# A constant tile of 64 bytes in place of 32: the left pools of an encoder block start 32 bytes later

## The chip, the cores and the metric

The kernel runs on one core of one Trainium2 chip. The metric is the device time of one execution in microseconds (us); lower is better. Three runs of the kernel before took 3334.75, 3335.2 and 3336.52 us, so the median is 3335.2 us.

## What is computed

One layer of a streaming encoder over x of 2048 tokens by 1024 features, all in float32. A projection feeds chunk-band attention and an RWKV-7 recurrence; the two are gated, merged and projected; then comes a feed-forward block. Cut to what matters here:

```python
h = rms_norm(x, pre_mix_g)
proj = h @ w_in                       # 1024 -> 5376
y_a = chunk_band_attention(q, k, v)   # from proj
y_b = rwkv7_time_mix(...)             # from proj
merged = sigmoid(gA) * (y_a @ proj_a) + sigmoid(gB) * (y_b @ proj_b)
x = x + rms_norm(merged @ w_out, post_mix_g)
hf = rms_norm(x, pre_ffn_g)
u = square(relu(hf @ w_up)) @ w_down  # 1024 -> 4096 -> 1024
x = x + rms_norm(u, post_ffn_g)
```

## The kernel before

**Products.** Every large product is made of three passes over operands that are split into a high and a low part (`split`, L76 and L77: ACT casts the high part, DVE subtracts it to get the low part). `mm3` (L85) issues, for each block of 128 along the contraction, high x high, high x low and low x high. Each pass is one MATMUL with a stationary operand of 128x128 (loaded by a LDWEIGHTS, the row PEld of the profile) and a moving operand of 128x512 float32. In a row of the profile the tile that is loaded as weights and the tile that streams stand in no fixed order, so the text says which is which.

**Order of the work.** The tokens are cut into four groups of 512. For each group the kernel runs the RWKV part, the attention part and the merge (`phase_rwkv`, `phase_attention`, `phase_merge`), all with the w_in, proj_a, proj_b and w_out products. Then the feed-forward runs in two halves of two groups each: `phase_up(0)`, `phase_down(0)`, `phase_up(1)`, `phase_down(1)`. Each of the four takes about 320 to 340 us.

**The up phase** (`phase_up`) works in 16 rows, each with two 128-column blocks of w_up on both halves of the contraction. A row is a scheme of seven products in place of eight, each of 12 matmuls (`product`): A11 and A12 against `bh`, `bl` (the normed input, `first_half`), and S2, S3, S1, S4, A22 against prepared combinations of the input, the tiles `t1`, `t2`, `t3`, `t4`, `b22`, each with an h and an l part. The weights (`a1h`, `s12h`, `s3h`, `s4h` and their l parts) are stationary; `bh`, `bl` and the t tiles stream. In each half the A11 and A12 products of the first eight rows are made ahead. In half 0 the rows from number 6 on also carry the steps of `residuals`, whose transposes (`ps_ht`, L1110) PE makes between products.

**The down phase** (`phase_down`) multiplies the squared activations by w_down: four plain blocks at each end (rows `ps_dn<-fop`: both operands lie in one tile) and between them 21 sums of products, each of 48 matmuls (rows `ps_dn<-fop,fop`: the stationary tile is `fop` from the pool z, the moving tile is `fop2` from the pool b).

**Where the tiles lie.** Pools are taken from one stack that grows upward (the left side) and one that grows downward from the top (`side="right"`). The left stack begins with the pool "const" (L160): `ident` (512 bytes in each partition), `g2c` (8 float32, 32 bytes) and `nhalf` (32 bytes). Everything in later left pools starts after these. On the left lie, among others, `whi` and `wlo` of the w_in stage, `hh`, `hl`, `mh`, `ml`, all t tiles, the pool z, and the pool b of half 0. On the right lie the operand pools of the up phase (`ops`, `ops1`: `a1`, `s12`, `s3`, `s4`), the pool `b1` (the place of `bh`, `bl` and of `fop2` in half 1), the attention's `ya`, and constants of the mixing stage.

These lines choose the side:

```python
            pt = u.enter_context(tc.tile_pool(name="ffp", bufs=2, space=PSUM, reuse_waits="tile"))
            self.phase_up(
                0, zp, rp, cb, pn, bpool(u, "ops", side="right"), 8, {},
...
                self.bp = bpool(ctx, "b1", side="right")
                self.sp = bpool(ahead, "ops1", side="right")
```

In the built program the steps between the blocks of one tile are 512 bytes for a stationary operand and 2048 bytes for a moving one, so all products of one pair of tiles have the same distance modulo 256. "Offset" below is the start of the moving operand minus the start of the stationary operand that is loaded while it streams (that of the following product), modulo 256.

Of the kernel before, what the change touches and what calls it, by code (L numbers as in the profile page):

```python
# [8 lines left out]
F32 = mybir.dt.float32  # L9
# [8 lines left out]
P = 128  # L18
D = 1024
KB = D // P  # L20
# [25 lines left out]
def advance(steps, n=None):  # L46

    while n is None or n > 0:
        if next(steps, steps) is steps:
            return  # L50
        n = n and n - 1


class Block:
# [102 lines left out]
    def constants(self, ctx, mixing):  # L157
        tc, nc, a = self.tc, self.nc, self.a
        keep = ctx.enter_context(tc.tile_pool(name="const", bufs=1))
# [1 line left out]
        dp = ctx.enter_context(tc.tile_pool(name="scratch", bufs=1, space=DRAM))  # L161
        self.ident = keep.tile([P, P], F32, name="ident")
        make_identity(nc, self.ident)
        self.g2c = keep.tile([P, KB], F32, name="g2c")
        self.nhalf = keep.tile([P, 8], F32, name="nhalf")
        nc.vector.memset(self.nhalf, -0.5)
        self.bones = cp.tile([P, P], F32, name="bones")
# [1351 lines left out]
    def run(self):  # L1519
        tc, e = self.tc, None  # L1520
        with ExitStack() as ctx, ExitStack() as mixing:
            e = mixing.enter_context
            consts = self.constants(ctx, mixing)
            advance(consts, 1)
            self.first = {}
            self.pd = ctx.enter_context(tc.tile_pool(name="pd", bufs=2, space=PSUM))
            self.wp = e(tc.tile_pool(name="w", bufs=2))
            self.hp = e(tc.tile_pool(name="h", bufs=1))
            with tc.tile_pool(name="p0", bufs=2, reuse_waits="tile") as sp, \
                 tc.tile_pool(name="p0p", bufs=2, space=PSUM, reuse_waits="tile") as pt:  # L1530
                self.phase_norm(0, sp, pt)
            advance(consts)
            self.order, self.feed = [], self.ahead()
            for g in range(self.NG):
                self.g = g
                self.phase_rwkv(g)
                self.phase_attention(g)
                with ExitStack() as c:
                    early = iter(())
                    if g == self.NG - 1:  # L1540
                        early = self.combinations(0, c.enter_context(tc.tile_pool(name="p1", bufs=1, reuse_waits="tile")), 2)
                    sp = c.enter_context(tc.tile_pool(name="p0", bufs=2, reuse_waits="tile"))
                    pt = c.enter_context(tc.tile_pool(name="p0p", bufs=2, space=PSUM, reuse_waits="tile"))
                    o = [sp.tile([P, D], F32, tag="o", bufs=GT, name=f"o{t}") for t in range(GT)]
                    self.phase_merge(g, o, self.after(g, sp, pt), early)
                    for t in range(GT):
                        self.nc.scalar.dma_start(self.od[g][t], o[t])
            mixing.close()
            e = ctx.enter_context
            zp = e(tc.tile_pool(name="z", bufs=2, reuse_waits="tile"))  # L1550
            rp = e(tc.tile_pool(name="raw", bufs=4, side="right", reuse_waits="tile"))
            cb = e(tc.tile_pool(name="cb", bufs=3, side="right", reuse_waits="tile"))
            pn = e(tc.tile_pool(name="ffpd", bufs=4, space=PSUM, reuse_waits="tile"))

            def bpool(ctx, name, **kw):
                return ctx.enter_context(tc.tile_pool(name=name, bufs=1, reuse_waits="tile", **kw))

            ahead = ExitStack()

            def nxt(loaded):  # L1560
                self.bp = bpool(ctx, "b1", side="right")
                self.sp = bpool(ahead, "ops1", side="right")
                load, parts = self.up_raw(rp), self.up_parts(self.sp)
                for i in range(2):
                    self.made[i] = self.up_first(i, load, parts)
                return self.first_half(2, self.bp, loaded)

            self.made = {}
            with ExitStack() as c:
                bp = bpool(c, "b")  # L1570
                advance(self.first_half(0, bp))
                with self.nc.allow_non_contiguous_dma(reason="one vector"):
                    self.nc.gpsimd.dma_start(self.g2c, self.a["pre_ffn_g"].rearrange("(k p) -> p k", p=P))
                with ExitStack() as u:
                    pt = u.enter_context(tc.tile_pool(name="ffp", bufs=2, space=PSUM, reuse_waits="tile"))
                    self.phase_up(
                        0, zp, rp, cb, pn, bpool(u, "ops", side="right"), 8, {},
                        lambda z, mp: self.residuals(z, mp, cb, pt),
                    )
                self.phase_down(0, zp, bp, rp, cb, pn, nxt)  # L1580
            self.phase_up(1, zp, rp, cb, pn, self.sp, 8, self.made)
            ahead.close()
            self.phase_down(1, zp, self.bp, rp, cb, pn)
# [44 lines left out]
```

## Time and profile before

| | |
|---|---|
| median of three runs | 3335.2 us |
| the profiled execution, its own time | 3334.86 us |
| its span, first to last instruction | 3333.2 us |
| mean granted TensorE clock | 0.994 |
| busy share of PE, PEld, DVE, ACT, POOL | 97%, 77%, 68%, 47%, 12% |

The span is the time between the first and the last instruction; 1.7 us of the execution lie outside it. PE is TensorE's products, PEld its weight loads, which run beside the products. DVE, ACT and POOL are the vector, scalar and GpSimd engines; SP only issues DMAs. A row of the listing by line and form gives the line, the engine, the operation, the output and input tiles, the shapes, the count, the busy time in us, the mean duration of one in ns, and the idle time of the engine just before these instructions with what ended it. Busy time is the union of the instructions' times: matmuls overlap in the records, so the busy time divided by the count is the step from one to the next, and the mean duration is longer than that step.

### The profile page before, as it was taken

To read this page: it belongs to the slowest core of one execution; us is meant where nothing else is said; L and a number is where in the kernel's file an instruction comes from. 1 tells how busy PE (TensorE), PEld (TensorE's weight loads), DVE (VectorE), ACT (ScalarE), POOL (GpSimd) and SP (SyncE) were. 2 spreads that over 40 slices of the span, in tenths; PEclk is the share of its full clock that TensorE was granted. 3 is DMA by queue.
4 is the path that set the end of the run, shared out by engine and by line. 5 is a ranking of instruction groups with operands and counts; after the bars stand their busy time and mean duration, and the time that the engine had idled before them with its cause. 6 is when DMAs were issued, how large, how long until landed. Compare 5 with 4: busy or idle time off the path is not lost. (4 is left out here: it accounts for less than half of the span.)

```text
span 3333.2 us, 49202 instructions
## 1 busy us (share of the span) xinstructions
PE 3236.2 (97%) x18945; PEld 2578.1 (77%) x18945; DVE 2271.5 (68%) x3782; ACT 1571.5 (47%) x2551; POOL 386.6 (12%) x757
## 2 busy tenths in 40 slices
PE   7999999999999999999999999999999999999998
PEld 6877787877777877778777777778788877887887
DVE  6784557765566765666775665777678978776687
ACT  4535534445644444645444635466443454454332
POOL 2110011101021011021111000133000111100001
PEclk9999999999999999999999999999999999999999
DMA  5224343225273234273224266566455564543443
GB/s 157 90 89 148 106 143 108 73 93 179 89 244 120 64 105 169 84 240 127 77 96 154 72 230 215 191 235 229 175 189 202 177 225 168 169 164 134 158 151 126
DMA packets 165874, 497.29 MB, mean 149 GB/s; under 512 B 18108, under 2 KB 26496, under 8 KB 160264
## 3 DMA queue, kind: packets, MB, share of 16 engines
q1 hardware_dynamic: 106740, 357.78, 32.5%
q0 software_dynamic: 22688, 77.61, 6.1%
q10 hardware_dynamic: 36212, 58.76, 4.8%
q8 instruction: 149, 2.44, 0.3%
q14 instruction: 85, 0.70, 0.1%
HBM read 365.08 MB, written 132.15 MB: 149 GB/s over the span
## 5 line engine op out<-in xcount | busy, mean ns | idle before, releaser
L85 PE MATMUL psd<-hh,whi 128*128 128x512 f32 x1344 | 542.0, 403 | 6.1 <-ACT whi L76 3.9
L85 PE MATMUL psd<-hl,whi 128*128 128x512 f32 x1344 | 534.8, 398 | 0.4 <-DVE hl L154 0.4
L85 PE MATMUL psd<-hh,wlo 128*128 128x512 f32 x1344 | 535.1, 398 | 0.0
L85 PE MATMUL ps_dn<-fop,fop 128*128 128x512 f32 x2016 | 464.5, 392 | 1.4 <-DVE y L1373 1.0
L76 ACT CAST whi<-wraw 128x1024 fp32r<-128x1024 f32 x232 | 243.3, 1049 | 460.7 <-PE psd L85 326.7
L85 PEld LDWEIGHTS ps_dn<-fop,fop 128*128 128x128 f32 x2016 | 378.2, 188 | 87.4 <-issue 2.1
L77 DVE TENSOR_TENSOR wlo<-wraw,whi 128x1024 fp32r<-128x1024 f32 x232 | 282.8, 1219 | 143.3 <-ACT whi L76 128.4
L85 PEld LDWEIGHTS psd<-hh,whi 128*128 128x128 f32 x1344 | 253.4, 189 | 62.6 <-ACT whi L76 4.6
L85 PEld LDWEIGHTS psd<-hh,wlo 128*128 128x128 f32 x1344 | 253.7, 189 | 56.0 <-issue 3.5
L85 PEld LDWEIGHTS psd<-hl,whi 128*128 128x128 f32 x1344 | 254.2, 189 | 48.9 <-issue 2.2
L76 ACT CAST fop<-ar 128x1024 fp32r<-128x1024 f32 x84 | 87.8, 1050 | 221.6 <-PE ps_dn L85 177.3
L85 PE MATMUL ps_dn<-fop 128*128 128x512 f32 x768 | 178.5, 393 | 1.6 <-DVE y L1373 1.2
L85 PEld LDWEIGHTS ps_dn<-fop 128*128 128x128 f32 x768 | 143.5, 188 | 36.0 <-DVE y L1373 3.1
L1373 DVE TENSOR_TENSOR y<-y,ps_dn 128x512 f32<-128x512 f32 x168 | 110.6, 685 | 50.2 <-PE ps_dn L85 49.9
L77 DVE TENSOR_TENSOR fop<-ar,fop 128x1024 fp32r<-128x1024 f32 x84 | 102.4, 1222 | 44.2 <-ACT fop L76 44.2
L904 DVE CUSTOM_DVE_ANT_0 sc<-bias,ps_s 128x640 f32<-128x640 f32 (+4 forms) x128 | 94.2, 736 | 51.6 <-PE ps_s L898 49.0
L909 ACT ACTIVATE sc<-sc,mn 128x640 f32<-128x640 f32 (+4 forms) x128 | 97.7, 763 | 35.4 <-DVE mn L904 30.9
L1029 PE MATMUL ps_o<-wlo,mh 128*128 128x512 f32 x256 | 103.1, 403 | 5.7 <-DVE wlo L77 5.7
L1029 PE MATMUL ps_o<-whi,ml 128*128 128x512 f32 x256 | 102.5, 400 | 0.0
L85 PE MATMUL ps_p<-yh,whi 128*128 128x512 f32 x256 | 101.1, 395 | 1.3 <-DVE th L995 1.3
L85 PE MATMUL ps_p<-yh,wlo 128*128 128x512 f32 x256 | 101.5, 396 | 0.2 <-DVE wlo L77 0.2
L1029 PE MATMUL ps_o<-whi,mh 128*128 128x512 f32 x256 | 101.6, 400 | 0.0
(384 smaller groups left out, 6819.2 us busy)
## 6 DMA issues: line engine op xcount, KB each, us to landing
wraw<-in_w_in_dram SPq DMA_DIRECT2D x168, 512.0 KB, 3.7
ar<-sd SPq DMA_DIRECT2D x42, 1024.0 KB, 4.6
wraw<-in_w_up_dram SPq DMA_DIRECT2D x80, 512.0 KB, 4.9
sd<-slots POOLq DMA_DIRECT2D x96, 256.0 KB, 5.2
qb<-in_w_down_dram SPq DMA_DIRECT2D x24, 1024.0 KB, 7.5
gd<-gate ACTq DMA_DIRECT2D x64, 256.0 KB, 3.4
wraw<-in_w_out_dram SPq DMA_DIRECT2D x32, 512.0 KB, 3.7
sd<-slots ACTq DMA_DIRECT2D x60, 256.0 KB, 4.5
```

The lines of the kernel that those rows point to most:

```text
L76: self.nc.scalar.copy(hi, src)
L77: self.nc.vector.tensor_tensor(lo, src, hi.bitcast(F32), ALU.subtract)
L85: mm = nc.tensor.matmul(ps, l, r, start=start and n == 0, stop=stop and n == last).ins
L904: nc.vector.tensor_tensor_reduce(sc[:, 0:n], bias[:, s0:640], pss[:, c0 : c0 + n], 1.0, 3.0e38, ALU.add, ALU.min, mn,)
L909: nc.scalar.activation(sc[:, 0:n], sc[:, 0:n], AF.Exp, scale=-1.0, bias=mn, accum_out=sm)
L1029: nc.tensor.matmul(ps[t], l[:, k, ts], r[:, k % 2], start=k == 0 and j == 0, stop=k == KB - 1 and j == 2)
L1373: self.add = nc.vector.tensor_tensor(dst, dst, ps, ALU.add).ins
```

## The change

The tile `g2c` gets 16 float32 in place of 8. Only its first eight are loaded and read; the rest is never touched. `ident` and `g2c` stay where they were. `nhalf` and every tile of every left pool start 32 bytes later. Nothing on the right side moves. The instructions of each of the five engines and their order are the same as before.

```diff
-        self.g2c = keep.tile([P, KB], F32, name="g2c")
+        self.g2c = keep.tile([P, 2 * KB], F32, name="g2c")
...
-                    self.nc.gpsimd.dma_start(self.g2c, self.a["pre_ffn_g"].rearrange("(k p) -> p k", p=P))
+                    self.nc.gpsimd.dma_start(self.g2c[:, 0:KB], self.a["pre_ffn_g"].rearrange("(k p) -> p k", p=P))
```

The offsets of the products with 512 columns, from the addresses in the two programs:

| products (moving, stationary) | count | offset before | offset after |
|---|---|---|---|
| w_in: hh, hl with whi, wlo | 4032 | 0 | 0 |
| proj_b: y from a left pool with whi, wlo | 384 | 0 | 0 |
| proj_a: y from the right pool ya with whi, wlo | 384 | 64 | 32 |
| w_out: whi, wlo with mh, ml, groups 0 to 2 | 576 | 128 | 128 |
| w_out, group 3 | 192 | 0 | 0 |
| up, half 0: bh, bl with a1, s12, s3 | 384 | 224 | 0 |
| up, half 1: bh, bl with a1, s12, s3 | 384 | 0 | 0 |
| up, both halves: t1, t2, t3, t4, b22 with s12, s3, s4 | 1920 | 224 | 0 |
| down, half 0: fop2 with fop | 1008 | 0 | 0 |
| down, half 1: fop2 with fop | 1008 | 32 | 0 |
| down, plain blocks, both halves | 768 | 0 | 0 |

The low-rank products of the RWKV part (64 of 512 columns) go from an offset of 64 to 96. The transposes, whose moving operand is `ident`, get an offset smaller by 32, since `ident` stays and their stationary operand moves. Modulo 64 alone, the pairs that stand at 224 or 32 before differ by 32 and agree after.

## The prediction

> **What bounds the kernel now.** I read the page first, then the busy time by stage, then the groups by line and form inside single stages. The page:
>
> ```profile
> span 3333.2 us, 49202 instructions
> PE 3236.2 (97%) x18945; PEld 2578.1 (77%) x18945; DVE 2271.5 (68%) x3782; ACT 1571.5 (47%) x2551; POOL 386.6 (12%) x757
> ```
>
> PE is busy in 97% of the span, and PEld, its weight loads, in 77%: most loads run while another product streams. So the step from one product to the next is the price of this kernel. The stages of the feed-forward, up and down of half 0, then of half 1:
>
> ```profile
> core 0: us, PE busy (x) PEld busy (x) DVE busy (x) ACT busy (x) POOL busy (x), PEclk, DMA share, GB/s
> 2031.90:2369.70 337.80, 326.57 (x1408) 260.17 (x1407) 241.63 (x319) 205.10 (x367) 69.20 (x128) 0.98 0.63 219
> 2369.70:2690.00 320.30, 316.26 (x1387) 259.32 (x1385) 263.40 (x320) 119.88 (x153) 26.75 (x44) 1.00 0.51 181
> 2690.00:3009.20 319.20, 314.74 (x1354) 253.99 (x1355) 226.87 (x304) 165.95 (x235) 26.05 (x49) 1.00 0.53 185
> 3009.20:3333.20 324.00, 314.07 (x1347) 252.05 (x1346) 245.15 (x294) 111.22 (x142) 11.46 (x24) 0.99 0.39 137
> ```
>
> PE stands idle for 4 to 11 us in each; DVE, the next, is busy for at most 263 of 320 us. A shorter step of the products would show in the span nearly in full.
>
> Is the step the same everywhere? First the same instruction in the same program in two places, the middle of the down phase of half 0 (2410 to 2640 us) and of half 1 (3050 to 3270 us):
>
> ```profile
> L85 PE MATMUL ps_dn<-fop,fop 128*128 128x512 f32 x984 | 223.8, 389 | 1.4 <-DVE y L1373 1.0 <-DVE v L1373 0.3
> L85 PE MATMUL ps_dn<-fop,fop 128*128 128x512 f32 x944 | 220.4, 395 | 0.0
> ```
>
> PE runs nothing but these here (and 24 plain ones in the first stretch), so busy time by count is the step: 223.8/984 = 227.4 ns in half 0, 220.4/944 = 233.5 ns in half 1, 6.1 ns more. The mean durations, 389 and 395, differ by as much. Half 0 also carries the combinations for the next half on DVE and DMA, so other traffic can't be why half 1 is the slower one. What differs is the place of the moving tile: on the left in half 0 (offset 0), on the right in half 1 (offset 32).
>
> Now the up phase of half 1, one stretch with one clock, where bh and bl lie on the right like the weights (offset 0) and the t tiles on the left (offset 224); then the same three forms in half 0, where bh and bl lie on the left too (offset 224):
>
> ```profile
> L85 PE MATMUL ps_u<-bh,a1h 128*128 128x512 f32 x80 | 31.3, 392 | 2.8 <-ACT z L1267 2.8
> L85 PE MATMUL ps_u<-bl,a1h 128*128 128x512 f32 x80 | 31.2, 390 | 0.0
> L85 PE MATMUL ps_u<-bh,a1l 128*128 128x512 f32 x80 | 31.1, 389 | 0.0
> L85 PE MATMUL ps_u<-t4h,s3h 128*128 128x512 f32 x64 | 25.3, 396 | 0.0
> L85 PE MATMUL ps_u<-t1l,s12h 128*128 128x512 f32 x64 | 25.3, 396 | 0.0
> ...
> L85 PE MATMUL ps_u<-bh,a1h 128*128 128x512 f32 x80 | 31.9, 399 | 0.0
> L85 PE MATMUL ps_u<-bl,a1h 128*128 128x512 f32 x80 | 31.6, 396 | 0.0
> L85 PE MATMUL ps_u<-bh,a1l 128*128 128x512 f32 x80 | 31.6, 395 | 0.0
> ```
>
> At offset 0 the mean is 389 to 392 ns, at 224 it is 395 to 399. Tiles, line and shapes are the same in the first three rows of each block; the side of bh and bl is not. Three pairs of rows thus say: products whose operands stand 32 bytes apart modulo 64 take 6 ns more each.
>
> Agreement modulo 64 is not the whole of it. The w_out products of group 2 (offset 128) and of group 3 (offset 0), minimum, median and maximum:
>
> ```profile
> L1029 PE MATMUL ps_o<-whi,ml x50: 390/394/482, 1469.7 to 1515.4; 128*128 128x512 f32 x50
> L1029 PE MATMUL ps_o<-whi,ml x56: 387/389/629, 1981.0 to 2021.0; 128*128 128x512 f32 x56
> ```
>
> Offset 128 agrees modulo 64 and has a median of 394, not 389. So I go by the offset modulo 256, and by that too the feed-forward comes out at 0 everywhere.
>
> **The change, part by part.** No instruction is added, removed or reordered, and the load into g2c keeps its eight columns.
>
> (a) Up, t products: 1920 go from offset 224 to 0, by the rows of half 1 from 396 to 390: 1920 x 6 ns = 11.5 us.
>
> (b) Up, half 0, bh and bl: 384 go from 224 to 0, from the 395 to 399 of half 0 to the 389 to 392 of half 1, about 6 ns: 2.3 us.
>
> (c) Down, half 1: 1008 go from 32 to 0, 233.5 to 227.4 ns: 6.1 us.
>
> Together 19.9 us. In (a) and (c) one thing has no row: afterwards the two tiles stand 256 bytes apart modulo 512, and the fast rows above stand at 0 modulo 512. If 256 costs what 128 costs at w_out (394 for 389), the gain is about a sixth of this. I take the full step, since the two rows at 32 and 224 lie just beside 256, on either side (288 and 224 modulo 512), and cost the same.
>
> (d) proj_a: 384 go from 64 to 32. In the merge of group 2 (1439 to 1469.9 us) they stand so:
>
> ```profile
> L85 PE MATMUL ps_p<-yh,whi 128*128 128x512 f32 x30 | 11.8, 395 | 0.0
> L85 PE MATMUL ps_p<-yh,wlo 128*128 128x512 f32 x30 | 11.8, 393 | 0.0
> L85 PE MATMUL ps_p<-yl,whi 128*128 128x512 f32 x30 | 11.7, 389 | 0.0
> ```
>
> Their mean is 392; at 32 the nearest row has 395 to 396. Bounds: 389 (a gain of 1.2 us) and 396 (a loss of 1.5 us). I take the loss, 1.5 us, since offset 32 has a row of its own. The 64 low-rank products lose between nothing and 64 x 6 ns; I take 0.4 us.
>
> (e) Transposes lose 32 bytes of offset against ident. Rows at offsets 192 and 32:
>
> ```profile
> L916 PE MATMUL ps_pt<-ident,sc 128*128 128x128 f32 x560 | 85.5, 279 | 2.0 <-ACT VV L857 1.2 <-DVE sc L912 0.8
> L516 PE MATMUL ps_bk<-ident,BK 128*128 128x128 f32 x128 | 21.6, 281 | 0.0
> ```
>
> 279 and 281 at quite different offsets: the offset costs a transpose at most 2 ns, either way, 1.1 us for the 560 of L916. I take nothing.
>
> (f) The w_in products and all left pairs keep their offsets, but now start at 32 modulo 64. The rows of bh in half 1 have both operands there and take 390, as the pair at 0 and 0 does (389). Nothing.
>
> (g) DVE and ACT: splits read and write left and right tiles in the same time, here with source and result at 0, then with the source at 32 modulo 64:
>
> ```profile
> L77 DVE TENSOR_TENSOR wlo<-wraw,whi 128x1024 fp32r<-128x1024 f32 x232 | 282.8, 1219 | 143.3 <-ACT whi L76 128.4 <-ACT yh L76 13.6
> L77 DVE TENSOR_TENSOR fop<-ar,fop 128x1024 fp32r<-128x1024 f32 x84 | 102.4, 1222 | 44.2 <-ACT fop L76 44.2
> ```
>
> Between 3 ns less and 3 ns more, and beside PE: nothing.
>
> (h) What is late next. PE's waits in the feed-forward:
>
> ```profile
> PE ps_ht L1110 <- ACT z L1102: 5.6, 4, 1.9
> PE ps_u L85 <- ACT z L1267: 4.4, 2, 2.8
> PE ps_u L85 <- DVE s3l L77: 3.4, 4, 1.8
> PE ps_dn L85 <- DVE y L1373: 2.2, 4, 1.0
> PE ps_u L85 <- ACT s12h L76: 1.8, 2, 0.9
> PE ps_u L85 <- ACT s3h L76: 1.6, 3, 1.2
> ```
>
> These 19 waits end when ACT or DVE are done. Where their work is not itself started by PE, the time that PE saves since the wait before comes back as a longer wait; a row of the up phase saves at most 84 x 6 ns = 0.5 us. Ends: nothing, and 19 x 0.5 = 9.5 us. I take four such rows, 2.0 us, since most of the 19 follow one another within a row, and PE's own last product starts the splits of s3h and s12h.
>
> Sum, against the profiled execution's own 3334.86 us (0.3 us below the median of 3335.2): 3334.86 - 19.9 + 1.5 + 0.4 + 2.0 = 3318.9, so 3319 us.
>
> **The rivals.** *DVE becomes the bound in the up phase.* Two stretches of it, in half 0 and in half 1:
>
> ```profile
> 2152.00:2170.00 18.00, 17.27 (x73) 13.34 (x72) 17.33 (x24) 8.93 (x14) 2.21 (x5) 1.00 0.58 209
> 2810.00:2830.00 20.00, 19.26 (x82) 14.90 (x81) 18.71 (x27) 11.61 (x18) 2.16 (x4) 1.00 0.47 175
> ```
>
> DVE is busy in 96% and 94% of them, and PE waits there. Against it: the stages as wholes have DVE at 72 and 71%. If all 9.5 us of (h) come back, the time is 3334.86 - 19.9 + 1.9 + 9.5 = 3326.4.
>
> *No change.* Either the offset of 256 modulo 512 is as dear as 32, or what I read as an effect of the offset belongs to the places of the tiles otherwise. Then only (d) is left: 3336.8. Against it stand the three pairs of rows.
>
> The Trainium skill, page "TensorE: Matmul & The Clock Gate", part 2, says that weights and the moving operand have two independent read ports, so that loading the next weights takes no bandwidth from the running product; by it the offset could not matter and the time would be 3334.9. The 389 and 395 of the same form speak against that. The page "SBUF — State Buffer", Specifications, gives lines of 16 bytes; 32 bytes keep every start on such a line, so by it too nothing would change, and the same rows disagree.
>
> *Slower.* What counts is not the distance but that each operand starts at a multiple of 64. Then half 1 of the down phase is slow because fop2 lies at 32, and the change makes slow what lies on the left: w_in (4032), w_out (768), proj_a and proj_b (768), down of half 0 (1008 and 384), 6960 products x 6 ns = 42 us, while the feed-forward rows that are slow stay so: 3377. It decides if a product with both operands at 32 is slow. The rows of bh and bl in half 1 are such, and have 389 to 392: strong evidence against.
>
> **How the numbers follow.** A measurement of this kernel can tell 0.2% from no change, 6.7 us: faster means under 3328.5. My forecast has a chance of 0.80, DVE as the bound 0.06, no change 0.09 (0.03 of it for the two pages), slower 0.05. The forecast's own ends: without any loss at waits, with (d) as a gain, 3334.86 - 19.9 - 1.2 = 3313.8, less some 2 us, since PEclk in the first stage is 0.98 and in the last 0.99, and such stretches of lower clock can come or go; above, with (h) in full, 3326.4. So 3312 to 3327, which takes in DVE as the bound as well; the rest is left out. Faster 0.85 (the forecast and nearly all of the first rival), same 0.10, slower 0.05.
>
> **What would show it right or wrong.** Right: the row of ps_dn<-fop,fop in half 1 at 389, with 227 to 228 ns a step; the t rows at 390; bh and bl in half 0 at 390 to 393; proj_a near 396; w_in unchanged. The up phases come out shorter by about 7 us (half 0) and 5 us (half 1), with the 2 us of (h) taken off, the down phase of half 1 by 6 us. Wrong: a t row still at 394 or more (the offset modulo 512 counts), waits of PE on DVE's s3l or ACT's z well above the 19 us listed, or w_in rows up by 6 ns.

## The result, and the profile after

The changed kernel takes 3319.95 us (median of 4 runs, 3316.37 to 3320.6), the kernel before on the same chip 3334.97 us (4 runs, 3328.33 to 3336.52). The ratio is 0.9957, with a 95% interval of 0.9939 to 0.9974: faster by 0.4%, 14 us by the ratio and 15 us by the medians. The profiled execution took 3319.51 us.

The page of the changed kernel:

```profile
span 3317.7 us, 49202 instructions
PE 3214.5 (97%) x18945; PEld 2576.2 (78%) x18945; DVE 2268.9 (68%) x3782; ACT 1571.4 (47%) x2551; POOL 384.9 (12%) x757
```

PE is busy 21.7 us less with the same 18945 products; DVE is busy 2.6 us less, ACT 0.1 us. Now down of half 1 (3041 to 3261 us), then up of half 1, then bh and bl in up of half 0:

```profile
L85 PE MATMUL ps_dn<-fop,fop 128*128 128x512 f32 x972 | 220.5, 389 | 0.0
...
L85 PE MATMUL ps_u<-t4h,s3h 128*128 128x512 f32 x64 | 24.9, 389 | 0.0
L85 PE MATMUL ps_u<-t1l,s12h 128*128 128x512 f32 x64 | 24.9, 389 | 0.0
...
L85 PE MATMUL ps_u<-bh,a1h 128*128 128x512 f32 x80 | 31.5, 393 | 0.0
L85 PE MATMUL ps_u<-bh,a1l 128*128 128x512 f32 x80 | 31.2, 390 | 0.0
L85 PE MATMUL ps_u<-bl,a1h 128*128 128x512 f32 x80 | 31.2, 389 | 0.0
```

The down step is 220.5/972 = 226.9 ns where it was 233.5, and the mean 389 where it was 395. These t rows went from 396 to 389, and bh and bl of half 0, which had 395 to 399, now have 389 to 393. The offset of 256 modulo 512, which no fast row of before had, is as fast as 0.

The mixing stage (all up to the first up product) and the two halves of the feed-forward, of the changed kernel:

```profile
core 0: us, PE busy (x) PEld busy (x) DVE busy (x) ACT busy (x) POOL busy (x), PEclk, DMA share, GB/s
0.00:2026.10 2026.10, 1961.61 (x13456) 1549.19 (x13457) 1294.77 (x2548) 969.49 (x1656) 251.06 (x513) 1.00 0.38 129
2026.10:2683.80 657.70, 635.85 (x2792) 519.84 (x2790) 503.95 (x638) 324.74 (x519) 96.32 (x172) 0.99 0.57 200
2683.80:3317.70 633.90, 617.03 (x2700) 507.13 (x2700) 470.21 (x598) 277.21 (x377) 37.48 (x73) 0.99 0.46 163
```

And of the kernel before, the same three windows:

```profile
0.00:2031.90 2031.90, 1964.54 (x13455) 1552.54 (x13456) 1294.42 (x2548) 969.35 (x1656) 253.13 (x513) 0.99 0.39 129
2031.90:2690.10 658.20, 642.94 (x2793) 519.59 (x2792) 505.14 (x638) 325.08 (x519) 96.05 (x172) 0.99 0.57 200
2690.10:3333.20 643.10, 628.71 (x2700) 505.94 (x2700) 471.92 (x598) 277.07 (x377) 37.41 (x73) 1.00 0.46 161
```

All these windows start late: their borders count from a moment 10.6 us ahead of the first instruction, where the profile's time starts. The first up product of the kernel before starts at 2021.3 us and not at 2031.9. The shift is the same in all kernels to 0.3 us. It leaves the length of half 0 and the differences between kernels as they are, but the mixing stage is some 10.6 us shorter than its window and half 1 as much longer. The lengths below go by the first up product of each half.

Before, half 0 took 658.2 us (first up product to the first of the next half) and half 1 took 653.7. So half 1 is shorter by 9.2 us, half 0 by 0.5 us only, although PE's busy time in its window fell by 7.1 us, and the mixing stage, where the forecast had a small loss, by 5.8 us. Both are what the experiments had to settle.

PE's waits in half 0 of the changed kernel, largest first:

```profile
PE ps_ht L1110 <- ACT z L1102: 9.0, 5, 3.4
PE ps_dn L85 <- DVE r L1246: 3.0, 1, 3.0
PE ps_u L85 <- DVE s3l L77: 2.7, 3, 1.7
PE ps_u L85 <- ACT s3h L76: 2.0, 2, 1.7
PE ps_u L85 <- ACT z L1267: 1.6, 1, 1.6
```

The wait for the residual steps' transposes (`ps_ht`) went from 5.6 to 9.0 us, and a new one of 3.0 us stands at the start of the down phase, where DVE is late.

The windows also show how a clock that comes and goes disturbs a mean. A stretch near the start of up in half 1 of the changed kernel, and two pieces of 3 us from it:

```profile
2683.70:2705.00 21.30, 18.59 (x73) 14.91 (x74) 12.06 (x12) 15.02 (x20) 0.22 (x1) 0.92 0.96 373
...
2696.70:2699.70 3.00, 3.00 (x8) 2.35 (x8) 3.00 (x3) 2.53 (x5) 0.00 (x0) 0.50 1.04 417
2700.70:2703.70 3.00, 3.00 (x15) 2.47 (x14) 1.36 (x2) 1.64 (x4) 0.00 (x0) 1.00 1.03 410
```

Soon after a wait of PE (2.7 us, for ACT's z) the granted clock is 0.50, and 8 products run in 3 us where 15 run at 1.00. The clock record of this trace has the half clock for 3.4 us here, which costs PE some 1.7 us. The rows of bh in this phase, whose offset did not change, had 389 to 392 ns and now have 396 to 400; from 2712 us on, after this stretch, they are at 389 to 390. In all the traces such stretches last 3.4 or 6.8 us (but for one at the very end), and many stand at other places from one profile to the next.

### The profile page after: what moved, and what is told of

The parts are those of the page before. It is cut to its first block, busy times and chain, and to the rows that moved or that the text cites. A ratio compares the mean times of both kernels' runs of the same rounds, so it can differ in the third digit from the quotient of the medians.

```text
span 3317.7 us, 49202 instructions
## 1 busy us (share of the span) xinstructions
PE 3214.5 (97%) x18945; PEld 2576.2 (78%) x18945; DVE 2268.9 (68%) x3782; ACT 1571.4 (47%) x2551; POOL 384.9 (12%) x757
## 5 line engine op out<-in xcount | busy, mean ns | idle before, releaser
L85 PE MATMUL ps_dn<-fop,fop 128*128 128x512 f32 x2016 | 457.8, 390 | 1.4 <-ACT fop L76 1.1
L77 DVE TENSOR_TENSOR wlo<-wraw,whi 128x1024 fp32r<-128x1024 f32 x232 | 282.8, 1219 | 144.9 <-ACT whi L76 129.9
```

The costliest lines, as they stand in the source:

```text
L77: self.nc.vector.tensor_tensor(lo, src, hi.bitcast(F32), ALU.subtract)
L85: mm = nc.tensor.matmul(ps, l, r, start=start and n == 0, stop=stop and n == last).ins
```

## The experiments

The theory on trial: the step from one product of 512 columns to the next depends on the offset modulo 256 of the streaming operand to the weights loaded meanwhile; the lowest step is at 0. The rivals: each operand's own start counts; the side counts; agreement modulo 64 is enough. And for the time: what takes back the gain in half 0, and is the shorter mixing stage an effect of the change.

Stages in us, from one profile of each kernel (mixing up to the first up product):

| kernel | mixing | half 0 | half 1 | median of runs | ratio to before, 95% interval |
|---|---|---|---|---|---|
| before | 2021.3 | 658.2 | 653.7 | 3334.97 | |
| changed | 2015.5 | 657.7 | 644.5 | 3319.95 | 0.9957, 0.9939 to 0.9974 |
| 32 bytes on the right | 2015.3 | 654.5 | 645.6 | 3317.41 | 0.9960, 0.9947 to 0.9972 |
| 96 bytes on the right | 2018.2 | 655.0 | 651.4 | 3327.17 | 0.9985, 0.9976 to 0.9994 |
| 160 bytes on the right | 2020.6 | 655.0 | 654.8 | 3330.54 | 0.9995, 0.9984 to 1.0005 |
| hh, hl moved by 32 | 2030.4 | 656.1 | 654.8 | 3343.79 | 1.0033, 1.0021 to 1.0045 |
| changed, two more pads | 2015.4 | 654.7 | 641.1 | 3312.84 | 0.9940, 0.9927 to 0.9952 |
| before, no residual steps | 2033.9 | 635.5 | 656.8 | 3322.28 | 0.9962, 0.9948 to 0.9976 |
| changed, no residual steps | 2031.1 | 627.5 | 642.8 | 3302.02 | 0.9898, 0.9882 to 0.9914 |
| two more pads, early loads | 2014.0 | 651.8 | 643.4 | 3313.42 | 0.9950, 0.9935 to 0.9966 |
| before, early loads | 2017.8 | 656.0 | 654.5 | 3334.20 | 0.9998, 0.9987 to 1.0009 |
| two more pads, gap | 2014.5 | 653.0 | 642.1 | 3311.60 | 0.9936, 0.9923 to 0.9948 |
| before, gap | 2016.2 | 656.2 | 655.2 | 3329.06 | 0.9990, 0.9981 to 0.9999 |

The first group of experiments shared 22 runs of the kernel before, with a median of 3333.06 us and a spread from 3324.97 to 3339.38. The ratios compare runs on one chip; a difference of medians can be a microsecond or two away from its ratio. A stage has one profile only, so single differences of 2 to 3 us between stages prove little.

### The same offsets, made from the other side

```diff
             zp = e(tc.tile_pool(name="z", bufs=2, reuse_waits="tile"))
+            pad = e(tc.tile_pool(name="pad", bufs=1, side="right")).tile([P, 8], F32, name="pad")
+            self.nc.gpsimd.memset(pad, 0.0)
```

> The kernel before, with 32 bytes put ahead of the feed-forward's right pools (one tile of 8 float32 and one memset on GpSimd, once). The left pools stay where they were, so nothing in the mixing stage moves; the feed-forward offsets become 0 modulo 256 as in the changed kernel, with the left operands at 0 and not at 32 modulo 64. Offset theory: the t rows, bh and bl of half 0 and the down rows of half 1 go to 389 to 390 ns, the down step of half 1 to 227 ns; about 20 us are saved in products, and the waits of PE in the feed-forward grow from 19.9 to about 28 us as they did with the change, so 10 us stay. If the 6 us by which the mixing stage was shorter in the changed kernel's profile were stretches at half clock that come and go, the time is 3323 to 3326 us; if they came from the change, they are missing here in every run too and the same time follows, but the mixing stage of the changed kernel is then shorter in all its runs. Rival, each operand's own start counts: the left operands haven't moved and the right ones leave 32 for 0 modulo 64, so all rows that were slow get fast as well, but bh in half 1, which had 32 and 32, would have been slow before, which it was not. Rival, the place of the tiles (left or right) counts: no row changes, 3335 us.

Down of half 1 and one t row of up in half 1:

```profile
L85 PE MATMUL ps_dn<-fop,fop 128*128 128x512 f32 x968 | 219.6, 389 | 0.0
...
L85 PE MATMUL ps_u<-t4h,s3h 128*128 128x512 f32 x60 | 23.3, 389 | 0.0
```

219.6/968 = 226.9 ns, with the left operands where they had been. So it is neither the left pools' own start nor the side, but the distance. The time, 3317.41 us, is lower than expected: the base of that chip is 3333.06, and 15.6 us stay by the medians (13 by the ratio), not 10.

The products of the mixing stage of this kernel are in order and in every address those of the kernel before, and so are those of the next two. In four profiles the same stage took 2021.3, 2015.3, 2018.2 and 2020.6 us. The 5.8 us of the changed kernel are within this spread. For the pair of before and changed the clock records show more: 23.9 us of this stage stand at half clock before and 10.2 us in the changed kernel. The difference is worth some 5 to 7 us, half of it at most and less where PE waits anyway. That is not all of the spread: the kernels with 32 and with 160 bytes have 13.7 us at half clock each, and differ by 5.3 us.

### Agreement modulo 64 that is none modulo 256

The same pad with 24 and with 40 float32 in place of 8.

> The same with 96 bytes. Both operands of the feed-forward agree modulo 64, but the offsets are 64 (up) and 192 (down of half 1) modulo 256. Modulo 64 is enough: the same rows and the same time as with 32 bytes, 389 to 390 ns. Modulo 256 decides: the rows come to about 391 to 392 ns, as proj_a at an offset of 64 had it before the change (mean 392), a step of about 229 ns in down of half 1; some 14 us saved in products and a part of it given back in waits, 3326 to 3330 us.

Down of half 1 (offset 192), two rows of up in half 1 (offset 64):

```profile
L85 PE MATMUL ps_dn<-fop,fop 128*128 128x512 f32 x944 | 220.4, 394 | 0.0
...
L85 PE MATMUL ps_u<-t4h,s3h 128*128 128x512 f32 x60 | 23.6, 393 | 0.0
L85 PE MATMUL ps_u<-t1l,s12h 128*128 128x512 f32 x57 | 22.2, 390 | 0.0
```

> The same with 160 bytes. Both operands agree modulo 64 and modulo 128, and the offsets are 128 modulo 256. Modulo 64 or 128 is enough: as with 32 bytes. Modulo 256 decides: the rows come to 394 to 395 ns, as w_out had it in groups 0 to 2, a step of 232 to 233 ns in down of half 1; under 2 us saved, 3332 to 3336 us.

Down of half 1 (offset 128) and a row of up in half 1:

```profile
L85 PE MATMUL ps_dn<-fop,fop 128*128 128x512 f32 x946 | 220.0, 395 | 0.0
...
L85 PE MATMUL ps_u<-t4h,s3h 128*128 128x512 f32 x59 | 23.3, 395 | 0.0
```

Steps: 233.5 ns at 192, 232.6 at 128; at 64 nearly all rows have 389 to 393, and from start to start the products of up take 229 ns. All these pairs agree modulo 64. Modulo 64 is not enough, and modulo 128 isn't either. One part of the expectation failed: 192 is no cheaper than 32, so in these rows the price is not the same on both sides of 0 (64 is measured on the up phase, 192 on the down phase). The times follow: 0.9985 where the up phases alone gain a part, no measurable change where nearly all rows stay slow, though 3330.54 us is a little below the 3332 to 3336 expected.

The traces settle one more point, whether the weights in use count or those that are loaded meanwhile. Nearly everywhere both lie at the same address modulo 256. They differ at 97 places in the plain blocks of the down phases, where a product has its own weights at offset 0 and the next ones, in another tile, elsewhere. From start to start these products take on average 234.4 ns (next weights at 32) and 232.6 (at 224) in the kernel before, 231.0 (64) and 232.4 (192) with 96 bytes, and 234.2 (128) with 160 bytes. In the changed kernel and with 32 bytes on the right, where the next weights are at 0 too, the same places take 227.0 and 226.8 ns. So it is the weights loaded meanwhile.

### The price in another stage

```diff
             self.hp = e(tc.tile_pool(name="h", bufs=1))
+            pad = self.hp.tile([P, 8], F32, name="pad")
+            self.nc.gpsimd.memset(pad, 0.0)
```

> The kernel before, with 32 bytes put ahead of hh and hl in their pool, so that the 4032 w_in products go from offset 0 to 32 (nearly all within one group of passes: 3683). With them 337 of proj_b go from 0 to 32 and w_out from 128 to 96 and, in group 3, from 0 to 224. The feed-forward stays as it was. Offset theory: the price is a property of TensorE's products and not of the feed-forward: the psd rows rise from 398 to 403 ns by 5 to 6 ns, 3683 x 5 to 6 = 18 to 22 us, with proj_b and w_out 22 to 27 us, of which PE's waits in the mixing stage take some in: 3352 to 3362 us. Rival, something of the feed-forward's own stages (their DMA or their split tiles) made the slow rows slow: no change, 3335 us.

The w_in rows of the kernel before, and of this one:

```profile
L85 PE MATMUL psd<-hh,whi 128*128 128x512 f32 x1344 | 542.0, 403 | 6.1 <-ACT whi L76 3.9
L85 PE MATMUL psd<-hl,whi 128*128 128x512 f32 x1344 | 534.8, 398 | 0.4 <-DVE hl L154 0.4
L85 PE MATMUL psd<-hh,wlo 128*128 128x512 f32 x1344 | 535.1, 398 | 0.0
...
L85 PE MATMUL psd<-hh,whi 128*128 128x512 f32 x1344 | 546.6, 407 | 3.3 <-DVE QA L843 2.6
L85 PE MATMUL psd<-hl,whi 128*128 128x512 f32 x1344 | 538.1, 400 | 0.0
L85 PE MATMUL psd<-hh,wlo 128*128 128x512 f32 x1344 | 537.4, 400 | 0.0
```

That is 10.2 us more. Its mixing stage:

```profile
0.00:2040.90 2040.90, 1978.81 (x13454) 1549.46 (x13455) 1294.11 (x2548) 969.47 (x1656) 255.58 (x514) 1.00 0.39 129
```

PE's busy time in it is 14.3 us above that of before (1964.54); 5.3 us of it come out of PE's idle time (67.4 us before, 62.1 now), and the stage is 9.0 us longer. The runs say 10.7 us. The sign is as expected, so the price belongs to the products and not to a stage. The time, 3343.79 us, stays below the 3352 to 3362 expected.

The rows understate the price. Their median goes from 389 or 390 ns to 394 to 396, and from start to start the median step goes from 227 to 234 ns, as in the down phase. The mean step, without the gaps over 260 ns, goes from 228.6 to 233.1 ns, some 18 us for the 4032 products: about a quarter of these steps were slow already at offset 0 (230 to 240 ns), for another reason that was not followed up. The rest of the difference is the clock: before, 23.9 us of this stage stand at half clock, here 10.2 us, so PE's busy time hides 5 to 7 us of the price. Why the runs show no more than 10.7 us is in part open; PE waits less in this kernel, as the expectation had it.

### Two more offsets brought to 0

```diff
+        pad = cp.tile([P, 8], F32, name="pad")
+        nc.vector.memset(pad, 0.0)
         self.gwo = cp.tile([C, 4], F32, name="gwo")
...
+            if g < self.NG - 1:
+                pad = cp.tile([P, 32], F32, name="pad2")
+                nc.gpsimd.memset(pad, 0.0)
             mh = cp.tile([P, KB, G], F32R, name="mh")
```

> The changed kernel with two more pads, each a small tile and one memset for each use: 32 bytes ahead of the attention's right pool, so that proj_a goes from an offset of 32 to 0, and 128 bytes ahead of mh and ml in groups 0 to 2, so that w_out goes from 128 to 0. Offset theory, by the steps measured so far: proj_a from 233.4 to 227 to 228.5 ns (384 x 5 to 6.4 = 1.9 to 2.4 us), w_out from 232.9 to 227 to 227.5 ns (576 x 5.5 = 3.2 us), 5.1 to 5.6 us of products saved; the merge waits little, so 4 to 5 us stay: 3314 to 3317 us on a chip where the changed kernel takes 3320. Rival, modulo 64 is what matters: w_out agrees modulo 64 already and its rows don't move, only proj_a gains, 2 us, 3318.

The merge of group 2 (1445.8 to 1467.3 us): proj_a, then w_out:

```profile
L85 PE MATMUL ps_p<-yl,whi 128*128 128x512 f32 x17 | 6.6, 389 | 0.0
L85 PE MATMUL ps_p<-yh,wlo 128*128 128x512 f32 x17 | 6.6, 389 | 0.0
L85 PE MATMUL ps_p<-yh,whi 128*128 128x512 f32 x16 | 6.3, 394 | 0.0
L1034 PE MATMUL ps_o<-whi,mh 128*128 128x512 f32 x16 | 6.2, 389 | 0.0
```

In the changed kernel both stood at 395. They come to 389 as every pair at offset 0 does, w_out too, which had agreed modulo 64 all along. (The 394 in the third row is one product of 472 ns beside a gap; the median of the row is 389.) The time is 3312.84 us, 0.9940 [0.9927, 0.9952]: better than the changed kernel (0.9957) by about the 5 us of products, though these two ratios are from different chips and their intervals overlap. The two profiles don't show the gain where it should lie: the mixing stage takes 2015.4 us here and 2015.5 in the changed kernel. But here 23.9 us of it stand at half clock, there 10.2 us, which is enough to hide 5 us. The steps from start to start, 227 to 228 ns on average in proj_a and w_out, are the surer sign.

### Half 0 without the residual steps

```diff
-        for g in range(2, self.NG):
-            for t in range(GT):
...
+        for g in range(2, self.NG):
+            for t in range(GT):
+                ts = slice(t * P, (t + 1) * P)
+                nc.gpsimd.dma_start(self.x1[g][ts], a["x"][g * G + t * P : g * G + (t + 1) * P])
+            for k in range(0, KB, 2):
+                nc.gpsimd.dma_start(self.ht[g][:, k : k + 2], self.ht[g - 2][:, k : k + 2])
+            yield
```

> The kernel before, with the residual sum and the norm of groups 2 and 3 left out: x1 of these groups is copied from x and their normed input from that of groups 0 and 1, by DMA, so that the up phase of half 0 carries no such steps on ACT, DVE and PE. This is the base for the next one. The up and down phases of half 0 took 657.8 us together in the profile of before; without the steps I expect PE's waits there (about 16 us with the steps' transposes) to fall by 8 to 12 us and these two phases to take 640 to 648 us, so 3317 to 3325 us in all.

> The changed kernel with the same part left out. In the profiles so far half 0 saved 8 us of product time in its up phase, but its two phases became shorter by only 0.5 to 3.8 us, while half 1, without such steps, kept 9 to 10 of 15. Theory 1, the residual steps take the gain back (ACT and DVE have to finish them in the same time, whatever PE does): without them the two phases of half 0 are shorter than in the kernel without them before by 7 to 8 us, and the whole program is 18 to 20 us faster than it. Theory 2, the waits belong to the seven products of a row themselves (DVE's splits of s3, s12) or to TensorE's clock: half 0 again keeps half or less, 2 to 4 us, and the whole is 13 to 16 us faster.

Half 0 of the kernel before and of the changed one, both without the steps:

```profile
2044.60:2680.10 635.50, 630.20 (x2728) 510.94 (x2727) 487.27 (x622) 282.78 (x383) 51.49 (x91) 1.00 0.52 180
```

```profile
2041.50:2668.90 627.40, 621.87 (x2727) 510.42 (x2725) 485.72 (x622) 282.24 (x382) 51.84 (x91) 1.00 0.53 182
```

PE is not busy for 5.3 us in the first and 5.5 us in the second, and the change keeps 8.1 us, all of what its products save there (1344 x 6 ns = 8.1). With the steps in place PE is idle in this window for 14.5 to 15.3 us in the five kernels whose products there are slow (before, 160 bytes, hh and hl moved, and before with early loads and with the gap of the next section), and for 17.8 to 21.9 us in the five whose products are fast. Half 0 without the steps is shorter than the 640 to 648 us expected. The medians of the runs differ by 20.3 us, where the kernels with the steps differ by 15.0; that points the same way, but is not clear of the noise of these runs. Theory 1 holds: in half 0 the residual steps take the gain back. (In both the mixing stage is 10 us or more longer than otherwise, 2033.9 and 2031.1 us; that is alike in the two and was not followed up.)

### Which link of the residual steps

First the loads. The next block's o goes to a second place and its x is loaded as soon as x is free:

```diff
-                nc.sync.dma_start(o, self.od[g][t])
-                nc.sync.dma_start(x, a["x"][g * G + t * P : g * G + (t + 1) * P])
-                yield
...
                 r = lengths(x, 1.0 / D, None)
+                if n + 1 < len(every):
+                    load_o(n + 1)
                 yield
                 nc.scalar.activation(o, x, AF.Copy, scale=r)
+                if n + 1 < len(every):
+                    load_x(n + 1)
                 yield
```

> The kernel with the two more pads, and the residual steps reordered: the next token block's o is loaded into a second place (the slots 6 and 7 of z) and its x as soon as x is free, two to four products ahead of their use and not one. Nothing is left out. Theory, it is ACT's wait for these loads (13.8 us in the changed kernel, with the splits for PE queued behind it) that gives the gain back in half 0: that wait goes to under 4 us, PE's waits for ps_ht from 9 us to under 3, and the two phases of half 0 from 654 us to 645 to 648, so 3304 to 3309 us. Rival, it is the chain of the steps on ACT, POOL and DVE (the wait of ACT on rs_r, of DVE on ACT): the loads come early and PE waits as before, 3311 to 3315 us.

> The kernel before, with the residual steps reordered in the same way and no pad. Theory of the loads: half 0 goes from 657.8 to 652 to 655 us, and the pair of this kernel and the padded one differs in half 0 by the full 8 us of products, 19 to 22 us in all with half 1, proj_a and w_out counted. Rival: half 0 differs by 4 us or less, as in the kernels without the reordering.

Against what the first expectation says, both kernels do change something: the first load into the second place overwrites slot 7 of z while row 7 of the up phase still needs it, so that row is computed from other numbers; the order of the work is as intended. ACT's longest waits in half 0 of the padded one, and PE's:

```profile
ACT sqo L1087 <- DMA ht<-hf: 10.8, 5, 4.3
ACT z L1119 <- POOL rs_r L132: 7.6, 7, 3.0
...
PE ps_ht L1129 <- ACT z L1119: 8.5, 3, 5.1
```

The wait of ACT for the loads of z, 13.1 us in the kernel without this edit, is gone. In its place ACT waits for its own stores, which hold the buffers (DMA ht<-hf: 4.0 before, 10.8 now), and PE's wait is 8.5 for 8.9 us. Half 0 takes 651.8 us, not 645 to 648, and the pair differs in it by 4.2 us, not 8. The theory of the loads fell.

Then the distance between ACT's scaling and PE's transposes:

```diff
                 nc.scalar.activation(o, x, AF.Copy, scale=r)
                 yield
+                yield
                 for h in range(2):
...
                     nc.gpsimd.dma_start(self.ht[g][:, h * 4 : h * 4 + 4, ts], f)
-                    yield
+                yield
```

> The kernel with the two more pads, and in the residual steps one empty step between ACT's scaling of the tokens and PE's transposes of them, while both groups of four transposes go into one step; the number of steps stays. PE then comes to the transposes two products (5.4 us) after ACT was given the scaling and not one. Theory, the distance of one product was too short for ACT, and the faster products made it shorter: PE's waits for ps_ht fall from 8.9 us to under 3, the two phases of half 0 from 654 to 646 to 650 us, 3305 to 3309 us. Rival, the whole chain of a token block (ACT, POOL, DVE, ACT and the buffers that its stores hold) takes longer than its seven products: the wait only moves, to the last block or to DVE and ACT at the start of the down phase, 3311 to 3315 us.

> The kernel before with the same edit to the residual steps and no pad. Theory: PE's waits for ps_ht fall from 5.6 us to under 2, half 0 from 657.8 to 652 to 655, 3328 to 3331 us; and the pair of this kernel and the padded one differs in half 0 by 6 to 8 us. Rival: as before within 3 us, and the pair differs by 4 us or less in half 0.

PE's waits in half 0 of the padded one:

```profile
PE ps_u L85 <- ACT s3h L76: 5.5, 3, 3.4
PE ps_u L85 <- DVE s3l L77: 2.4, 3, 1.3
PE ps_dn L85 <- DVE y L1379: 2.2, 2, 1.4
PE ps_ht L1116 <- ACT z L1107: 2.0, 1, 2.0
```

The wait for ps_ht fell from 8.9 to 2.0 us as the theory had it, and the wait for s3h rose from 1.9 to 5.5, with 2.2 more at the down phase. Half 0 takes 653.0 us in place of 654.7, and the pair differs in half 0 by 656.2 - 653.0 = 3.2 us. In the kernel before, the same edit brings the wait for ps_ht from 5.6 to 1.4 us and half 0 from 658.2 to 656.2. The rival was right: most of the wait only moves. With this edit the kernel takes 3311.6 us, 0.9936 [0.9923, 0.9948], the fastest one here with nothing left out; against the one without the edit (0.9940) that is no difference that these runs can tell.

So it is shown that the residual steps as a whole take back half of half 0's gain or more (kept: 0.5, 3.7, 4.2 and 3.2 us in four pairs, 8.1 without them), and that neither their loads nor the distance to the transposes is the link alone. Which chain of ACT, POOL, DVE and stores sets the pace is open. Half 1, which has no such steps, loses something too: PE's idle time in its window is 14.4 us before and 16.9 in the changed kernel, 13.9 to 15.6 in the other kernels with slow products and 15.7 to 17.4 in those with fast ones.

## Why the prediction was right, and where it was not

**(a) to (c), the products.** Right, in place and size. 1920 + 384 + 1008 products got 6 to 7 ns faster. PE's busy time in the windows of the feed-forward fell by 18.8 us, where 19.9 were forecast: 7.1 in half 0 and 11.7 in half 1. (The other 2.9 us of the 21.7 lie in the mixing stage, which has fewer stretches at half clock in this profile.) The assumption without a row, that 256 modulo 512 is as good as 0, held.

**The rule for the offset.** Modulo 256 was right and modulo 64 was not, by the kernels with 96 and 160 bytes. All starts here are multiples of 32 bytes; nothing finer was tried.

**(d), proj_a.** Right. The products of group 2's merge, before and after:

```profile
L85 PE MATMUL ps_p<-yh,whi 128*128 128x512 f32 x17 | 6.7, 395 | 0.0
L85 PE MATMUL ps_p<-yh,wlo 128*128 128x512 f32 x17 | 6.7, 393 | 0.0
L85 PE MATMUL ps_p<-yl,whi 128*128 128x512 f32 x17 | 6.6, 389 | 0.0
```

```profile
L85 PE MATMUL ps_p<-yh,wlo 128*128 128x512 f32 x18 | 7.1, 395 | 0.0
L85 PE MATMUL ps_p<-yh,whi 128*128 128x512 f32 x17 | 6.7, 395 | 0.0
L85 PE MATMUL ps_p<-yl,whi 128*128 128x512 f32 x17 | 6.7, 395 | 0.0
```

The mean goes from 392.3 to 395, 384 x 2.7 = 1.0 us by the means; from start to start the mean step goes from 229.2 to 233.3 ns, 1.6 us. 1.5 were forecast. The 64 low-rank products went from a mean of 392 to 397 ns, 0.3 us, where 0.4 were forecast.

**(e) and (g).** Right: the transposes of L916 have 279 ns before and after, and the splits 1219 and 1221.

**(f), the left pairs that moved together.** Right: the w_in row of hh and whi has 403 as before, with both operands at 32 modulo 64. That was the point at which the slower rival decided.

```profile
L85 PE MATMUL psd<-hh,whi 128*128 128x512 f32 x1344 | 541.7, 403 | 4.5 <-ACT KK L849 2.4
```

**(h), the waits.** Mis-sized. The forecast took 2.0 us between the ends of 0 and 9.5. In the profile PE's waits in half 0 alone grew from 15.0 to 21.1 us, and over the whole feed-forward PE's idle time grew by 9.1 us in the changed kernel and by 4.8 to 5.7 us in four other pairs. The step that failed is the choice of four rows. In half 0 the waits belong to the residual steps, which run through ten rows with ACT, POOL and DVE; without them the idle time there does not grow. The reading that each product which PE finishes sooner brings it sooner to the next link of their chain fits this, but no run shows the link. The upper end, each wait growing by a row's saving, was nearer for the changed kernel. One sign that the prediction named for being wrong came in part: PE's waits in the feed-forward went from 19.9 to 28.2 us, 3.4 us of it at ps_ht on ACT's z, while those on s3l did not grow.

**The phases.** The down phase of half 1 became 6.3 us shorter, as forecast (6). The up phases became 4.8 and 2.9 us shorter, where 7 and 5 were forecast, and the down phase of half 0, where no change was forecast, became 4.2 us longer (2.5 us with the offsets made from the right), with the wait of 3.0 us at its start and a stretch at half clock in it. The prediction's own windows of these phases start 10.6 us late like those above. With the right borders PE stands idle for 3 to 11 us in each, where it read 4 to 11, and nothing else in its argument changes.

**The total.** 3319 was forecast and 3319.95 measured. Part of that closeness is luck: in the profiled execution the loss at the waits is larger than forecast, and the mixing stage is 5.8 us shorter, which needs no effect of the change, since the same stage, unchanged, took 2015.3 to 2021.3 us. The feed-forward by itself became 9.7 us shorter in the changed kernel and 11.8 us with the offsets made from the right; the runs measured 15.0 and 15.6 us by the medians, and the interval of the ratio goes from 9 to 20 us.

**The two pages.** By the Trainium skill, page "TensorE: Matmul & The Clock Gate", part 2, weights and moving operand are read through two independent ports, and by the Trainium skill, page "SBUF — State Buffer", Specifications, SBUF has lines of 16 bytes, of which a shift of 32 bytes is a whole number. The down step of 233.5 against 226.9 ns for the same tiles, moved by 32 bytes, disagrees with what was drawn from both; the measurement decides.

## What to carry to other kernels

Where TensorE is busy all the time, compare the mean duration of the same product in two places of the program; 6 ns in 395 showed a placement effect that no wait shows. A pad of 32 to 128 bytes that brings the streaming operand and the weights to the same address modulo 256 gave 0.4 to 0.6% here, and since pools stack, one pad breaks other pairs, so list the offsets of all pairs before and after. Count of such a gain only what the chains beside PE let through: where ACT, POOL and DVE run a chain of their own between the products, half of it or more came back as waits.

## What was not expected of the hardware

- The price of an offset is uneven: by the median from start to start about 227 ns a step at 0, 229 at 64, and 232 to 234 at 32, 96, 128, 192 and 224.
- The weights that count are those of the next product: 231 to 234 ns where only they lie at another offset.
- The same program on one core varies more than three runs suggest: 22 runs of the kernel before went from 3324.97 to 3339.38 us, and the same mixing stage from 2015.3 to 2021.3. Stretches of 3.4 or 6.8 us at half clock stand at different places in each profile and go with a part of it: among the 17 runs of the kernel before on the last chip the six with a mean granted clock of 0.997 or 0.998 took 3326 to 3331 us, the three with 0.993 or 0.994 took 3336 to 3339.
